# Where attention weights are normalised in a hybrid decoder layer: from GpSimd to VectorE

## The chip, the cores and the metric

One core of a Trainium2 chip. The metric is the device time of one execution in microseconds (us). A difference of about 0.2% (1.2 us) is what a measurement of this kernel can tell from no change; this bound is used throughout. Engines are named as the profile names them: PE (TensorE; PEld is its weight load), DVE (VectorE), ACT (ScalarE), POOL (GpSimd), SP (SyncE, which issues most transfers).

## What is computed

One decoder layer for 512 tokens of width 1024, in fp32. Token mixing projects the normalised input into two groups of eight heads of 64: group A is block-sparse attention (with 512 tokens and blocks of 256, every query sees all earlier keys), group B is a sliding window of 128 with a learned sink per head. The outputs are joined, projected, normalised and gated; a squared-ReLU MLP of 4096 hidden units follows. What matters here is the softmax of one head and one block of 128 queries:

```python
# group A: causal, up to 512 keys
p = softmax(q @ k.T * scale + bias)
# group B: two blocks of 128 keys, and one more column, the sink, whose weight is thrown away
p = softmax(concatenate([where(allowed, q @ k.T * scale + bias, -inf), sink]))[..., :-1]
out = p @ v
```

## The kernel before, in words

The layer is three stages in the span. Up to about 80 us the first normalisation, the conditioning vectors and the first q and k projections. From 80 to 232 us attention, with the remaining projections and the output projection mixed in. From 232 us the residual, the second normalisation and the MLP, which is a nearly unbroken run of matmuls to the end.

**Attention.** There are 64 blocks (`blocks`, line 822): eight pairs of heads, two heads each, four blocks `i` of 128 queries. A block has 128, 256, 384 or 512 keys in the 32 blocks of group A, and 128 (i = 0) or 256 in the 32 of group B (`keys`, line 627). The loop at line 825 is a pipeline over steps k: step k issues the transposes of block k-3, the scores of block k, the normalisation of block k-2, the bias step and the exponentials of block k-1, and the split of the transposed weights of block k-5 or so. For each block:

- `scores` (line 631), PE: two matmuls (lines 641, 642) into a PSUM bank. A tile `w` is taken for the weights, one of four in turn. For group B, POOL copies the head's negated sink into the column behind the last key of `w` (line 640).
- `add_bias` (line 644), DVE: one fused instruction adds the bias strip to the scores, writes `w` and keeps the row minimum in `st` (line 649).
- `exps` (line 653), ACT: the exponential in place, with the row sum in `st` (line 656); with the sink's column for group B.
- `normalise` (line 659): DVE takes the reciprocal of the sum (line 662, 128x1); then POOL multiplies `w` by it (line 663).
- `transposes` (line 665), PE: `w` by 128 columns into PSUM (line 672), the only reader of the normalised weights.
- `weights` (line 674): ACT copies the transposed weights out of PSUM in a rounded form (line 686), DVE takes the difference as the low part (line 687). `output` (line 689) multiplies them with v on PE (line 699); `evacuate` (line 703) uses ACT, DVE and, for a pair of heads, POOL (lines 709 to 715).

**What runs beside it.** `side_steps` (line 786) sums 24 tiles of conditioning weights (512 KB each) in 48 instructions on DVE (lines 282, 284), two a tile, spread over the steps by `side_at` (line 795). Weights are split in a high part by ACT (line 83) and a low part by POOL, in some cases by DVE (line 85). Filler matmuls (projections, then chunks of the output projection, `y_chunk`, line 753) are dealt out between the blocks.

**What sets the order.** PE's order is written out by hand: it is the order of the program (line 821). The other engines are ordered when the program is built, by a planner that simulates the engines and takes what is ready; each engine then runs its queue in that order. Filler and side work is tied behind the latest bias step on DVE and the latest exponential on ACT (`anchor`, `behind`, lines 470 to 477), so it can't be taken earlier; nothing ties it to a latest place.

Of the kernel before, what the change touches and what calls it, by code (L numbers as in the profile page):

```python
# [24 lines left out]
ALU = mybir.AluOpType  # L25
# [7 lines left out]
NHA = 8  # L33
# [13 lines left out]
def layer_kernel(ctx, tc, x, c_col, ada_c, ada_r, bada_col, bada_row, gain_col, gain_row, w_in0, w_in1, w_in2,  # L47
                 w_out, w1, b1_col, w2, b2_row, rel, sinks, onehot, out):
    nc = tc.nc
# [10 lines left out]
    def bank(name):  # L60
        return psum.tile([P, 512], F32, tag="ps", name=name)
# [121 lines left out]
    sink_t = const.tile([P, NHB], F32, name="sink_t")  # L183
# [157 lines left out]
    for i in range(NT):  # L341
        n = DM if i < NT - 1 else S
# [68 lines left out]
    for kc in range(KC):  # L411
# [3 lines left out]
        for k in range(18):  # L415
# [18 lines left out]
            w, h = (w0[kc][0], hh) if k < 6 else (w0[kc][1], hh) if k < 12 else (w0[kc][0], hl)  # L434
# [174 lines left out]
    class Head:  # L609
# [21 lines left out]
        def scores(self, i):  # L631
            k0, nk = self.keys(i)
            n = nk * P
            kk = slice(k0 * P, (i + 1) * P)
            q = self.q[:, i * P:(i + 1) * P]
            self.s[i] = s_ps = bank(f"s{self.h}_{i}")
            tag, bufs = ("stash", 2) if step[0] > 23 and step[0] % 3 == 2 else ("w", 4)
            self.w[i] = w = apool.tile([P, 512], F32, tag=tag, name=f"w{self.h}_{i}", bufs=bufs)
            if self.swa:
                nc.gpsimd.tensor_copy(w[:, n:n + 1], sink_t[:, self.h - NHA:self.h - NHA + 1])  # L640
            nc.tensor.matmul(s_ps[:, :n], q, self.kh[:, kk], start=True, stop=False)
            nc.tensor.matmul(s_ps[:, :n], q, self.kl[:, kk], start=False, stop=True)

        def add_bias(self, i):
            n = self.keys(i)[1] * P
            w = self.w[i]
            self.st[i] = st = small.tile([P, 3], F32, tag="st", name=f"st{self.h}_{i}", bufs=8)
            init = sink_t[:, self.h - NHA:self.h - NHA + 1] if self.swa else BIG
            anchor["dve"] = nc.vector.tensor_tensor_reduce(  # L649
                w[:, :n], self.s[i][:, :n], self.strip[:, 512 - n:], scale=1.0, scalar=init, op0=ALU.add, op1=ALU.min,  # L650
                accum_out=st[:, 0:1]).ins
# [7 lines left out]
        def normalise(self, i):  # L659
            n = self.keys(i)[1] * P  # L660
            w, st = self.w[i], self.st[i]
            nc.vector.reciprocal(st[:, 2:3], st[:, 1:2])  # L662
            nc.gpsimd.tensor_scalar(w[:, :n], w[:, :n], st[:, 2:3], 1.0, op0=ALU.mult, op1=ALU.mult)  # L663

        def transposes(self, i):
            if self.swa and i % 2:
# [368 lines left out]
    for f in range(3, NF):  # L1035
        if f < 5:
            ws.make("both")
        w = ws.get(0 if f < 4 else 1)
# [20 lines left out]
    for f in range(NF - LAST):  # L1059
        w = ws.get()  # L1060
# [106 lines left out]
```

## Time and profile before

| | us |
|---|---|
| median of 3 runs (621.97 to 622.14) | 622.05 |
| the profiled execution's own time | 623.07 |
| its span, first to last instruction | 621.3 |
| PE, DVE, ACT, POOL busy in the span | 580.3, 315.2, 279.2, 321.6 |
| line 663 on POOL, 64 instructions | 38.2 |
| line 640 on POOL, 32 instructions | 11.4 |

The profile is of one execution. Busy time is the time in which an engine has an instruction running; a wait is idle time in front of an instruction, put down to what released it. [...] The execution profiled took 1.8 us more than its span and 1.0 us more than the median of the runs.

### The profile page before, as it was taken

How to read it: one execution, taken by the hardware profiler on the slowest of the kernel's cores; microseconds unless marked ns; L12 is line 12 of the kernel's file. 1: busy time of each engine (PE TensorE's matmuls, PEld its weight loads, DVE VectorE, ACT ScalarE, POOL GpSimd, SP SyncE). 2: the span in 40 equal slices, each digit the busy share in tenths (PEclk: the TensorE clock that was granted, in tenths of full speed). 3: DMA queues.
4: the chain of work that ended last, by engine and by line, in shares of the span. 5: the costliest groups of instructions: out<-in, count | busy, mean ns of one | idle time of the engine just before them, and what ended most of it. 6: DMA issues, size and time to landing. Idle time of an engine off the chain costs nothing.

```text
span 621.3 us, 8137 instructions
## 1 busy us (share of the span) xinstructions
PE 580.3 (93%) x2829; PEld 482.0 (78%) x2829; DVE 315.2 (51%) x599; ACT 279.2 (45%) x532; POOL 321.6 (52%) x333
## 2 busy tenths in 40 slices
PE   2789989999897999999999999999999999999994
PEld 0477889887675888898888888788888888888883
DVE  4646679999998756535255555522401111111037
ACT  4624776578667545773233332233522333323122
POOL 1514234666898653636555555655544444446432
PEclk9969999999998999999999999999999999999998
DMA  8990569686466207734244432223232233333105
GB/s 308 419 383 1 189 129 260 128 170 224 140 185 207 84 1 270 236 106 149 89 136 136 146 125 99 80 93 101 71 112 89 100 103 102 102 101 116 56 17 186
DMA packets 29677, 89.31 MB, mean 144 GB/s; under 512 B 3427, under 2 KB 7587, under 8 KB 29636
## 3 DMA queue, kind: packets, MB, share of 16 engines
q1 hardware_dynamic: 28816, 86.52, 43.5%
q10 hardware_dynamic: 692, 2.23, 0.9%
q8 instruction: 22, 0.36, 0.3%
q14 instruction: 19, 0.16, 0.1%
q0 software_dynamic: 128, 0.05, 0.1%
HBM read 84.56 MB, written 4.22 MB: 143 GB/s over the span
## 4 chain that ended last, share of the span: by engine, by line
PE 55%; DVE 2%; ACT 2%; DMA 1%; issue 1%; POOL 0%; DVEq 0%; POOLq 0%; ACTq 0%; SPq 0%
PE u L97 9%; PE u L98 9%; PE u L96 9%; PE y L98 9%; PE y L97 9%; PE y L96 9%; DVE zg L1090 1%; ACT hf L379 1%; DMA x<-in_x 1%; ACT h2h L378 0%; DVE x L933 0%; DMA out_x<-zg 0%; ACT sq L208 0%; PE adarow L299 0%; POOL zg L1087 0%
## 5 line engine op out<-in xcount | busy, mean ns | idle before, releaser
L85 POOL TENSOR_TENSOR wlo<-raw,whi 128x512 fp32r<-128x512 f32 (+1 forms) x140 | 192.4, 1393 | 157.7 <-ACT whi L83 157.2
L83 ACT ACTIVATE whi<-raw 128x1024 fp32r<-128x1024 f32 (+5 forms) x87 | 80.7, 934 | 130.8 <-PE u L97 108.9
L97 PE MATMUL u<-h2l,whi 128*128 128x512 f32 (+1 forms) x280 | 104.2, 372 | 1.2 <-POOL h2l L380 1.1
L96 PE MATMUL u<-h2h,whi 128*128 128x512 f32 (+1 forms) x280 | 104.7, 374 | 0.0
L98 PE MATMUL u<-h2h,wlo 128*128 128x512 f32 (+1 forms) x280 | 103.8, 371 | 0.0
L97 PE MATMUL y<-wlo,ring_h2h 128*128 128x512 f32 x232 | 90.2, 389 | 0.0
L98 PE MATMUL y<-whi,ring_h2l 128*128 128x512 f32 x232 | 90.2, 389 | 0.0
L96 PE MATMUL y<-whi,ring_h2h 128*128 128x512 f32 x232 | 90.1, 389 | 0.0
L284 DVE SCALAR_TENSOR_TENSOR adaacc<-adar,c_act,adaacc 128x512 f32<-128x512 f32 x56 | 66.7, 1191 | 0.0
L97 PEld LDWEIGHTS u<-h2l,whi 128*128 128x128 f32 x280 | 52.7, 188 | 11.3 <-POOL h2l L380 1.7
L96 PEld LDWEIGHTS u<-h2h,whi 128*128 128x128 f32 x280 | 52.7, 188 | 9.2 <-ACT whi L83 0.2
L98 PEld LDWEIGHTS u<-h2h,wlo 128*128 128x128 f32 x280 | 52.7, 188 | 9.2
L663 POOL TENSOR_SCALAR w<-w,st 128x128 f32<-128x128 f32 (+2 forms) x64 | 38.2, 599 | 38.2 <-DVE st L662 32.8
L97 PEld LDWEIGHTS y<-wlo,ring_h2h 128*128 128x128 f32 x232 | 43.5, 188 | 9.1
L96 PEld LDWEIGHTS y<-whi,ring_h2h 128*128 128x128 f32 x232 | 43.5, 188 | 9.0
L98 PEld LDWEIGHTS y<-whi,ring_h2l 128*128 128x128 f32 x232 | 43.5, 188 | 9.0
L656 ACT ACTIVATE w<-w,st 128x128 f32<-128x128 f32 (+3 forms) x64 | 33.4, 522 | 28.2 <-DVE st L649 26.1
L85 POOL TENSOR_TENSOR w0lo<-w0raw,w0hi 128x384 fp32r<-128x384 f32 x16 | 17.2, 1095 | 29.3 <-ACT w0hi L83 29.3
L672 PE MATMUL p<-ident,w 128*128 128x128 f32 x136 | 25.9, 279 | 6.4 <-POOL w L663 5.9
L672 PEld LDWEIGHTS p<-ident,w 128*128 128x128 f32 x136 | 17.3, 142 | 13.4 <-POOL w L663 9.6
L686 ACT ACTIVATE pth<-p 128x384 fp32r<-128x384 f32 (+3 forms) x48 | 22.2, 466 | 10.1 <-PE p L672 9.6
L687 DVE TENSOR_TENSOR ptl<-p,pth 128x384 fp32r<-128x384 f32 (+3 forms) x48 | 25.0, 523 | 0.8 <-ACT pth L686 0.6
(222 smaller groups left out, 1093.9 us busy)
## 6 DMA issues: line engine op xcount, KB each, us to landing
raw<-in_w SPq DMA_DIRECT2D x63, 512.0 KB, 3.3
adar<-in_ada_r SPq DMA_DIRECT2D x32, 512.0 KB, 4.1
ada<-in_ada_c SPq DMA_DIRECT2D x16, 512.0 KB, 8.6
woraw<-in_w_out SPq DMA_DIRECT2D x8, 512.0 KB, 4.4
raw<-in_w_in SPq DMA_DIRECT2D x7, 512.0 KB, 6.7
w0raw<-in_w_in SPq DMA_DIRECT2D x8, 384.0 KB, 9.1
strip<-vec SPq DMA_DIRECT2D x24, 128.0 KB, 4.1
xn<-in_x SPq DMA_DIRECT2D x4, 512.0 KB, 10.0
```

Of the source, the lines that this page charges most:

```text
L83: nc.scalar.activation(hi[:, a:b], src[:, a:b], AF.Copy)
L85: return eng.tensor_sub(lo[:, a:b], src[:, a:b], f32(hi[:, a:b])).ins
L96: nc.tensor.matmul(ps, lh, rh, start=start, stop=False, **kw)
L97: nc.tensor.matmul(ps, lh, rl, start=False, stop=False, **kw)
L98: nc.tensor.matmul(ps, ll, rh, start=False, stop=stop, **kw)
L284: nc.vector.scalar_tensor_tensor(a, w, c_act[:, j:j + 1], a, op0=ALU.mult, op1=ALU.add)
L379: nc.scalar.activation(hf[:, :n], tp, AF.Identity, bias=sh_col, scale=a_col)
L656: anchor["act"] = nc.scalar.activation(w[:, :m], w[:, :m], AF.Exp, bias=st[:, 0:1], scale=-1.0, accum_out=st[:, 1:2]).ins
L663: nc.gpsimd.tensor_scalar(w[:, :n], w[:, :n], st[:, 2:3], 1.0, op0=ALU.mult, op1=ALU.mult)
L672: nc.tensor.transpose(p_ps[:, (c0 + j) * P:(c0 + j + 1) * P], self.w[i][:, j * P:(j + 1) * P], ident)
L686: nc.scalar.activation(dst(self.pth), src, AF.Copy)
L687: nc.vector.tensor_sub(dst(self.ptl), src, f32(dst(self.pth)))
```

## The change

In `scores` the copy of the sink's column by POOL goes. In `add_bias` the same copy is issued on DVE, directly ahead of the bias step. In `normalise` the multiplication is issued on DVE, directly behind the reciprocal. Shapes, operands and everything else stay.

```diff
--- before.py
+++ after.py
@@ -636,8 +636,6 @@
             self.s[i] = s_ps = bank(f"s{self.h}_{i}")
             tag, bufs = ("stash", 2) if step[0] > 23 and step[0] % 3 == 2 else ("w", 4)
             self.w[i] = w = apool.tile([P, 512], F32, tag=tag, name=f"w{self.h}_{i}", bufs=bufs)
-            if self.swa:
-                nc.gpsimd.tensor_copy(w[:, n:n + 1], sink_t[:, self.h - NHA:self.h - NHA + 1])
             nc.tensor.matmul(s_ps[:, :n], q, self.kh[:, kk], start=True, stop=False)
             nc.tensor.matmul(s_ps[:, :n], q, self.kl[:, kk], start=False, stop=True)
 
@@ -646,6 +644,8 @@
             w = self.w[i]
             self.st[i] = st = small.tile([P, 3], F32, tag="st", name=f"st{self.h}_{i}", bufs=8)
             init = sink_t[:, self.h - NHA:self.h - NHA + 1] if self.swa else BIG
+            if self.swa:
+                nc.vector.tensor_copy(w[:, n:n + 1], init)
             anchor["dve"] = nc.vector.tensor_tensor_reduce(
                 w[:, :n], self.s[i][:, :n], self.strip[:, 512 - n:], scale=1.0, scalar=init, op0=ALU.add, op1=ALU.min,
                 accum_out=st[:, 0:1]).ins
@@ -660,7 +660,7 @@
             n = self.keys(i)[1] * P
             w, st = self.w[i], self.st[i]
             nc.vector.reciprocal(st[:, 2:3], st[:, 1:2])
-            nc.gpsimd.tensor_scalar(w[:, :n], w[:, :n], st[:, 2:3], 1.0, op0=ALU.mult, op1=ALU.mult)
+            nc.vector.tensor_scalar(w[:, :n], w[:, :n], st[:, 2:3], 1.0, op0=ALU.mult, op1=ALU.mult)
 
         def transposes(self, i):
             if self.swa and i % 2:
```

## Rows read from the trace of the kernel before

**Rows 1.** Busy time by stretch of the span, all engines of the core:

```profile
core 0: us, PE busy (x) PEld busy (x) DVE busy (x) ACT busy (x) POOL busy (x), PEclk, DMA share, GB/s
...
90.00:110.00 20.00, 18.74 (x129) 18.16 (x130) 19.86 (x59) 14.53 (x42) 9.21 (x12) 1.00 0.86 212
110.00:150.00 40.00, 39.99 (x214) 33.24 (x212) 38.39 (x90) 27.84 (x71) 27.10 (x30) 1.00 0.75 181
150.00:190.00 40.00, 34.36 (x200) 28.37 (x201) 39.40 (x107) 29.25 (x77) 34.35 (x54) 1.00 0.56 167
190.00:200.00 10.00, 7.06 (x32) 4.70 (x31) 8.59 (x22) 7.55 (x15) 7.94 (x11) 0.89 0.59 188
200.00:210.00 10.00, 10.00 (x53) 8.70 (x52) 6.68 (x23) 3.90 (x12) 6.95 (x14) 0.77 0.62 184
210.00:232.00 22.00, 22.00 (x131) 18.88 (x131) 14.26 (x40) 13.60 (x32) 12.75 (x25) 1.00 0.01 1
```

**Rows 2.** Waits of PE from 80 to 232 us (total, times, longest in us):

```profile
PE p L672 <- POOL w L663: 5.9, 8, 1.6
PE y L97 <- POOL wo_hl L85: 1.7, 2, 1.3
```

**Rows 3.** Timeline, all engines, around one SWA block (start us, us taken):

```profile
168.87 0.19 ACT L656 ACTIVATION_READ_ACCUMULATOR w<-w,st 128x1 f32 x1
...
169.23 0.67 DVE L687 TENSOR_TENSOR ptl<-p,pth 128x512 fp32r<-128x512 f32 x1
...
169.82 0.67 DVE L710 TENSOR_TENSOR of<-o,of 64x512 f32<-64x512 f32 x1
...
170.52 0.69 DVE L528 SCALAR_TENSOR_TENSOR q<-proj,q 64x512 fp32r<-64x512 f32 x1
...
171.05 1.29 POOL L85 TENSOR_TENSOR wlo<-raw,whi 128x512 fp32r<-128x512 f32 x1
...
171.24 0.35 DVE L649 CUSTOM_DVE_ANT_0 w<-s,strip,sink_t 128x128 f32<-128x128 f32 x1
...
171.52 1.36 DVE L284 SCALAR_TENSOR_TENSOR adaacc<-adar,c_act,adaacc 128x512 f32<-128x512 f32 x1
...
172.80 0.15 DVE L662 RECIPROCAL st<-st 128x1 f32<-128x1 f32 x1
...
173.06 0.48 POOL L663 TENSOR_SCALAR w<-w,st 128x256 f32<-128x256 f32 x1
...
173.59 0.44 PE L672 MATMUL p<-ident,w 128*128 128x128 f32 x2 [0.63 <-POOL w L663]
```

**Rows 4.** POOL's groups by shape from 80 to 200 us, the change's two lines:

```profile
L663 POOL TENSOR_SCALAR w<-w,st 128x256 f32<-128x256 f32 x20 | 11.1, 556 | 7.5 <-DVE st L662 4.0 <-PE v L97 3.0
L640 POOL COPY w<-sink_t 128x1 f32<-128x1 f32 x21 | 9.0, 438 | 1.7 <-PE p L672 1.7
...
L663 POOL TENSOR_SCALAR w<-w,st 128x512 f32<-128x512 f32 x8 | 7.5, 940 | 8.1 <-DVE st L662 8.0
L663 POOL TENSOR_SCALAR w<-w,st 128x128 f32<-128x128 f32 x13 | 6.7, 518 | 12.5 <-DVE st L662 12.4
L663 POOL TENSOR_SCALAR w<-w,st 128x384 f32<-128x384 f32 x8 | 5.2, 648 | 6.1 <-DVE st L662 4.6 <-PE p L672 1.4
```

**Rows 5.** VectorE's groups by shape, 0 to 30 us, line 337:

```profile
L337 DVE TENSOR_SCALAR xn<-xn,s2x 128x128 f32<-128x128 f32 x4 | 1.1, 286 | 1.2 <-POOL s2x L213 1.2
```

**Rows 6.** Instructions of line 282 (ns: least, median, most):

```profile
L282 DVE TENSOR_SCALAR adaacc<-adar,c_act x8: 477/896/1512, 51.3 to 319.3; 128x512 f32<-128x512 f32 x8
```

**Rows 7.** Timeline of VectorE, a producer and the instruction that reads it:

```profile
15.47 0.15 DVE L256 TENSOR_TENSOR mods<-adaps,bada_c 128x2 f32<-128x2 f32 x1
15.66 0.21 DVE L259 TENSOR_SCALAR mods<-mods,gain_c 128x1 f32<-128x1 f32 x1
```

**Rows 8.** Timeline of VectorE, four small instructions that don't depend:

```profile
163.50 0.57 DVE L259 TENSOR_SCALAR mods<-mods,gain_c 128x1 f32<-128x1 f32 x4
```

**Rows 9.** Busy time of line 85 from 80 to 200 us, VectorE, then POOL:

```profile
80.00:200.00 120.00, 8.72 (x10) 29.07 (x22) 0.99 0.67 177
```

**Rows 10.** VectorE's groups by shape from 80 to 200 us, the side products:

```profile
L284 DVE SCALAR_TENSOR_TENSOR adaacc<-adar,c_act,adaacc 128x512 f32<-128x512 f32 x39 | 38.5, 987 | 0.0
...
L282 DVE TENSOR_SCALAR adaacc<-adar,c_act 128x512 f32<-128x512 f32 x4 | 3.3, 847 | 0.0
```

**Rows 11.** Instructions of line 284 (ns: least, median, most):

```profile
L284 DVE SCALAR_TENSOR_TENSOR adaacc<-adar,c_act,adaacc x56: 724/1059/1881, 54.0 to 395.5; 128x512 f32<-128x512 f32 x56
```

## The prediction, made before the changed kernel was run

> **What bounds the kernel now.** I read the busy time by stretch first, because shares over the whole span mix attention with an MLP that the change doesn't touch. Attention has two parts [rows 1]. From 110 to 150 us PE is busy 39.99 of 40 us: the matmuls set the pace. From 150 to 190 us PE is busy 34.36 of 40, and from 190 to 200 us 7.06 of 10; its granted clock then falls to a mean of 0.89 and 0.77 in the two stretches around 200 us. What must be seen beside it is DVE: 19.86 of 20 us, 38.39 of 40, 39.40 of 40. From 90 to 190 us it has 2.35 us free in 100. POOL is busy too, 34.35 of 40 us, but only late.
>
> The waits of PE name POOL: 5.9 us in 8 waits are put down to line 663 [rows 2]. The timeline shows what lies behind such a wait [rows 3]. ACT has the row sum ready at 169.06 us (168.87 + 0.19). The reciprocal starts at 172.80, 3.74 us later, because DVE first works off its queue: lines 687, 710, 528, 649, 284. POOL then starts 0.11 us after the reciprocal and takes 0.48 us, and PE goes on at 173.59, having idled 0.63 us. So the releaser is POOL, but 3.74 of the 4.53 us from row sum to transposes are DVE's queue. In attention DVE is the engine without room, and after 232 us nothing is left that could make up for a late end, as PE runs matmuls nearly without a gap.
>
> A second thing is in the same rows. Line 284 on DVE took 1.36 us there; its least is 0.72 [rows 11]. It began at 171.52, in the middle of POOL's line 85 (171.05 to 172.34), and ended 0.54 us after that. DVE instructions with their operands in SBUF wait out the POOL instruction that they meet.
>
> **What is removed.** POOL loses line 663, 30.5 us in 49 instructions from 80 to 200 us, and line 640, 9.0 us in 21 [rows 4]. POOL doesn't set the pace, so by itself this gives nothing; what it gives is shorter waits of DVE, below. The hop to POOL goes from the chain of a block: 0.11 + 0.48 us become about 0.04 + 0.35. That is latency, and with a queue of 3.7 us in front of it, it doesn't matter.
>
> **The multiplication on DVE.** No row shows this line on DVE; the nearest are the same operation of the same form on other tiles: 286 ns for 128x128 [rows 5], 477 ns for 128x512 when nothing interferes [rows 6]; between them I go in a straight line, 0.35 and 0.41 us for 256 and 384. An independent instruction starts about 0.08 us before the end of the one in front: four of 0.20 us stand in 0.57 us [rows 8]. So each costs the queue 0.20, 0.27, 0.33 or 0.40 us, and the 13, 20, 8 and 8 of the stretch [rows 4] 2.6 + 5.4 + 2.6 + 3.2 = 13.8 us. The multiplication reads the reciprocal just in front of it. A reader starts 0.04 us behind its producer's end [rows 7] and not 0.08 us before it, 0.12 us more; for 49 that is 5.4 us with the rounding, unless the planner puts another instruction between. Bounds 13.8 and 19.2 us; I take the middle, 16.5, since both orders will occur.
>
> [...]
>
> **The sink's copy on DVE.** No row shows it; the nearest are 128x1 instructions, one every 0.12 us [rows 8]. 21 of them make 2.5 us; 1.5 if each costs only the 0.07 us between a reciprocal and the start of an independent instruction behind it, 6.7 if each also meets POOL as below. It waits for the `w` buffer to be free, as the bias step behind it did already, so no wait is new. I take 2.5.
>
> **Meeting POOL.** The multiplication moves from POOL onto DVE as an instruction that POOL can hold up: line 282, the same operation, has a median of 896 ns against a least of 477 [rows 6]. What stays on POOL from 80 to 200 us is line 85, 29.1 us in 22 [rows 9], and some 10 us of other work (POOL's 78.6 us from 90 us on [rows 1] less lines 85, 663 and 640): 39 of 120 us. Half a piece of line 85 is 0.66 us; the rest is in shorter pieces, and I take 0.60 for all. One in three meets a piece and waits 0.60 us, so 0.20 us each, 9.8 us for 49. Bounds: nothing, if they never meet, and 0.42 us each, 20.6 us, if they fare like line 282's median.
>
> **What DVE gets back.** Lines 284 and 282 took 38.5 us in 39 and 3.3 us in 4 [rows 10]; at their least, 0.72 and 0.48, that would be 28.2 and 1.9, so 11.7 us were waits for POOL. A wait goes with the length of what is met: lines 663 and 640 (0.62 and 0.44 us long) carry 30.5 x 0.31 + 9.0 x 0.22 = 11.5, the rest 39 x 0.60 = 23.4, so a third, 3.8 us, goes. Bounds 0 and 11.7.
>
> **The sum.** 16.5 + 2.5 + 9.8 - 3.8 = 25.0 us more work on DVE by 200 us, less its 2.35 us of free time: 23 us later. Two things come back. The 1.7 us in which PE waits for POOL's halves of the output weights [rows 2] end, as POOL is less loaded. [...] Of these 5.1 us I take 4: 19 us. The other 15 multiplications and 11 copies fall after 200 us, where DVE is busy 6.68 of 10 and 14.26 of 22 us [rows 1]; their 15 x 0.34 + 11 x 0.12 = 6.4 us I cost at nothing, since 11 us are free there and PE sets the pace; without that cover they'd be 6 us more. The delay then runs to the end one to one: from a profiled time of 623.07 us to 642, from the median of 622.05 us to 641. With all low ends the sum is 13.8 + 1.5 + 0 - 11.7 - 2.35 - 5.1 = -3.9 us, with all high ends 19.2 + 6.7 + 20.6 - 2.35 = 44.
>
> **The rivals.** *Faster: the hop was the limit.* If DVE's queue isn't what holds PE, the shorter chain ends PE's 5.9 us of waits for line 663 and the 3.4 us of low clock: 9.3 us less, 613 us. It decides at the transposes of the group B blocks from 150 us on, and needs that DVE has room there. For it: the waits name POOL, and POOL is busy 34.35 of 40 us. Against it: the 3.74 us in which the row sum lay ready [rows 3]. 0.07. [...]
>
> *Covered.* The planner orders DVE anew. If it pushes the side products of lines 282 and 284, which nobody needs before the second normalisation, behind the blocks' own work, or if nearly all waits for POOL vanish, the added work finds room: -4 to +3 us, 622. Against it: the side product starts right behind a bias step [rows 3], as soon as its tie allows. 0.08, of which 0.05 lies within 0.2%.
>
> *Much slower.* The multiplications meet POOL as line 282's median does, 10.8 us more, and PE, idle more often, falls to its lower clock twice more at the 3.4 us that it cost here: 19 + 10.8 + 6.8, 658 us. For it: 7.06 busy of 10 us stand in front of the fall [rows 1]; against it: 34.36 of 40 did not bring one. 0.11.
>
> **How the numbers follow.** The forecast, DVE's queue paces attention, has 0.74 and spans +5 to +33 us by its own bounds taken half way. The range 627 to 655 us leaves out the faster case, the covered one and half of the heaviest, 0.2 in all. Faster by over 0.2%: 0.07. Within: 0.05. Slower: the rest, 0.88.
>
> **What would show it.** In the changed profile DVE should be busy 98% from 90 us to past 210, line 663 on DVE should have means over the uncontended 0.29 to 0.48 us, with 0.1 to 0.3 us of waiting in each. PE should wait at line 672 for DVE, some 25 us in many small waits instead of 5.9, and the first transposes of group B's last head should come some 19 us later, with the MLP unchanged in length. POOL's line 85 should stay near its length. I'd be wrong if DVE had free time between 110 and 190 us, if line 284 stood far behind its bias steps, or if the end of attention stayed near 232 us.

## The result and the profile after

The changed kernel takes 639.04 us (median of 4 runs, 638.91 to 639.55) against 622.01 us for the kernel before beside it: 17.0 us more, a ratio of 1.0289 with a 95% interval from 1.0259 to 1.0319. (The ratio is formed from all runs and is not the quotient of the two medians, which is 1.0274; the same holds below.) The profiled execution took 639.05 us, its span is 637.3.

The first view is the page's busy time by engine (us, share of the span, instructions).

```profile
PE 584.1 (92%) x2829; PEld 482.7 (76%) x2829; DVE 338.5 (53%) x695; ACT 279.8 (44%) x532; POOL 273.6 (43%) x237
```

DVE reads 338.5 us against 315.2 before, POOL 273.6 against 321.6: VectorE has 23.3 us more work, POOL 48.0 us less. The same stretches as in [rows 1], now of the kernel after (PEclk is the clock that TensorE was granted, as a share of its full one):

```profile
core 0: us, PE busy (x) PEld busy (x) DVE busy (x) ACT busy (x) POOL busy (x), PEclk, DMA share, GB/s
...
90.00:110.00 20.00, 17.49 (x115) 15.75 (x116) 19.43 (x56) 12.17 (x34) 2.92 (x3) 1.00 0.85 209
110.00:150.00 40.00, 36.98 (x199) 30.46 (x198) 39.48 (x94) 24.28 (x61) 14.66 (x14) 1.00 0.66 152
150.00:190.00 40.00, 32.22 (x176) 26.62 (x175) 39.43 (x122) 26.44 (x67) 13.67 (x12) 0.96 0.50 147
190.00:200.00 10.00, 7.95 (x45) 6.04 (x43) 9.81 (x27) 6.36 (x18) 5.19 (x5) 1.00 0.50 138
200.00:210.00 10.00, 6.21 (x30) 4.99 (x31) 9.81 (x29) 6.59 (x16) 1.85 (x2) 0.91 0.42 123
210.00:232.00 22.00, 20.40 (x115) 16.45 (x114) 21.39 (x73) 13.11 (x32) 8.20 (x9) 0.96 0.43 141
```

VectorE was full until 190 us before and had 3.32 of 10 and 7.74 of 22 us free behind it. It is full to 232 us now: 9.81 of 10, 9.81 of 10, 21.39 of 22. TensorE, at 39.99 of 40 us from 110 to 150 before, is at 36.98: it waits there now too. The granted clock is at 0.50 from 177.5 to 180.9 and from 208.3 to 211.7 us, where it was at 0.50 from 197.8 to 204.6 us before, and at 1.00 elsewhere in attention; back-to-back matmuls of 512 columns mostly start 0.43 us apart at 0.50 and 0.23 at 1.00. By the means of the stretches that costs an estimated 40 x 0.04 + 10 x 0.09 + 22 x 0.04 = 3.4 us of matmul time, as much as the 10 x 0.11 + 10 x 0.23 = 3.4 us before [rows 1], so the clock doesn't account for the difference.

How much of the 16.0 us of span arose in attention is read from a step that both chains of waits contain, the first residual step behind attention (line 933). Before, then after:

```profile
249.36 2.82 DVE x L933 x2
```

```profile
265.71 2.46 DVE x L933 x2
```

16.35 us of delay are there at 265.71 us, and 16.0 us at the end of the span. The MLP kept its length. Who holds TensorE in attention (total, times, longest):

```profile
PE p L672 <- DVE w L663: 12.8, 12, 2.2
PE p L672 <- DVE st L662: 2.6, 1, 2.6
PE y L97 <- DVE wloo L85: 1.8, 1, 1.8
PE p L672 <- DVE w L648: 1.7, 1, 1.7
```

The 5.9 us in 8 waits of [rows 2] have become 12.8 + 2.6 + 1.7 us in 14 waits, now put down to VectorE. The halves of the output weights, 1.7 us behind POOL before, are waited for behind VectorE's own splitting (1.8 us). VectorE's groups by shape over attention, 80 to 260 us:

```profile
L284 DVE SCALAR_TENSOR_TENSOR adaacc<-adar,c_act,adaacc 128x512 f32<-128x512 f32 x40 | 33.6, 840 | 0.0
L663 DVE TENSOR_SCALAR w<-w,st 128x256 f32<-128x256 f32 x32 | 15.7, 491 | 0.3
...
L663 DVE TENSOR_SCALAR w<-w,st 128x384 f32<-128x384 f32 x8 | 6.1, 762 | 0.1
L663 DVE TENSOR_SCALAR w<-w,st 128x128 f32<-128x128 f32 x16 | 6.0, 374 | 0.1
...
L663 DVE TENSOR_SCALAR w<-w,st 128x512 f32<-128x512 f32 x8 | 4.7, 585 | 0.1
L648 DVE COPY w<-sink_t 128x1 f32<-128x1 f32 x32 | 4.4, 138 | 0.0
...
L282 DVE TENSOR_SCALAR adaacc<-adar,c_act 128x512 f32<-128x512 f32 x4 | 3.9, 1008 | 0.0
```

Four things are in it. The 64 multiplications take 15.7 + 6.1 + 6.0 + 4.7 = 32.5 us. At the durations without interference of the prediction (0.29, 0.35, 0.41, 0.48 us) they would take 16 x 0.29 + 32 x 0.35 + 8 x 0.41 + 8 x 0.48 = 23.0; the other 9.5 us, 0.15 us each, are meetings with POOL. The trace bears that out: the 42 that overlap no instruction of POOL take at most 0.29, 0.36, 0.41 and 0.49 us, and the 22 that overlap one carry the excess. The 32 copies take 4.4 us, of which about half overlaps with what is behind them. Line 284 is down to 840 ns in the mean, from 987 [rows 10]: 40 x 0.147 = 5.9 us that VectorE got back from POOL, as 28 of the 40 now overlap no instruction of POOL, where 8 did not before. Line 282 got nothing back (1008 ns in the mean, 847 before [rows 10]). An instruction's time overlaps with that of its neighbours (behind the multiplication at 205.10 us, which takes 0.35 us, the next instruction starts at 205.36), so these rows add up to more than the 23.3 us of busy time.

### The profile page after: what moved, and what is told of

Read it like the earlier page. It is cut to its first block, busy times and chain, and to the rows that moved or that the text cites. A ratio compares the mean times of both kernels' runs of the same rounds, so it can differ in the third digit from the quotient of the medians.

```text
span 637.3 us, 8053 instructions
## 1 busy us (share of the span) xinstructions
PE 584.1 (92%) x2829; PEld 482.7 (76%) x2829; DVE 338.5 (53%) x695; ACT 279.8 (44%) x532; POOL 273.6 (43%) x237
## 4 chain that ended last, share of the span: by engine, by line
PE 53%; DVE 2%; ACT 2%; DMA 1%; issue 1%; POOL 0%; DVEq 0%; POOLq 0%; ACTq 0%; SPq 0%
PE u L97 9%; PE u L98 9%; PE u L96 9%; PE y L98 9%; PE y L97 9%; PE y L96 9%; DVE zg L1090 1%; DMA x<-in_x 1%; ACT hf L379 1%; ACT h2h L378 0%; DMA out_x<-zg 0%; DVE x L933 0%; ACT sq L208 0%; PE adarow L299 0%; POOL zg L1087 0%
## 5 line engine op out<-in xcount | busy, mean ns | idle before, releaser
L97 PEld LDWEIGHTS u<-h2l,whi 128*128 128x128 f32 x280 | 52.7, 188 | 11.5 <-POOL h2l L380 1.9
L284 DVE SCALAR_TENSOR_TENSOR adaacc<-adar,c_act,adaacc 128x512 f32<-128x512 f32 x56 | 60.8, 1086 | 0.1
L672 PE MATMUL p<-ident,w 128*128 128x128 f32 x136 | 26.1, 281 | 18.3 <-DVE w L663 12.8
L663 DVE TENSOR_SCALAR w<-w,st 128x128 f32<-128x128 f32 (+2 forms) x64 | 32.0, 507 | 0.5
L1027 DVE TENSOR_TENSOR ring_h2l<-rsq_hl,ring_h2h 128x512 fp32r<-128x512 f32 x8 | 5.5, 694 | 38.0 <-ACT ring_h2h L1026 38.0
```

The costliest lines, as they stand in the source:

```text
L97: nc.tensor.matmul(ps, lh, rl, start=False, stop=False, **kw)
L284: nc.vector.scalar_tensor_tensor(a, w, c_act[:, j:j + 1], a, op0=ALU.mult, op1=ALU.add)
L663: nc.vector.tensor_scalar(w[:, :n], w[:, :n], st[:, 2:3], 1.0, op0=ALU.mult, op1=ALU.mult)
L672: nc.tensor.transpose(p_ps[:, (c0 + j) * P:(c0 + j + 1) * P], self.w[i][:, j * P:(j + 1) * P], ident)
```

## The experiments

Each kernel ran beside the kernel before on the same chip. The kernel before had medians of 621.3 to 621.5 us there, its single runs from 617.8 to 624.4. The intervals reach 0.2 to 0.35%, some 1.3 to 2.1 us, to either side.

**One part at a time.** The copy alone (the multiplication stays on POOL):

```diff
     def scores(self, i):
...
-            if self.swa:
-                nc.gpsimd.tensor_copy(w[:, n:n + 1], sink_t[...])
     def add_bias(self, i):
...
+            if self.swa:
+                nc.vector.tensor_copy(w[:, n:n + 1], init)
```

> Only the sink's copy goes to VectorE, the multiplication stays on POOL. If VectorE's amount of work is the cost: 32 copies at 0.07 us between starts are 2.4 us more, less about 1 us of waits for POOL's copies that end: 0 to +2 us against before. If POOL's late queue was what held TensorE (its copies took 9.0 us from 80 to 200 us): 3 to 5 us faster than before.

Measured: 619.78 us, ratio 0.9977 (0.9955 to 1.0). That lies below the range of the first theory and above that of the second; it is at the edge of no change. The gain of 3 to 5 us is just excluded (the interval ends at 2.8 us).

The multiplication alone:

```diff
     def normalise(self, i):
...
-            nc.gpsimd.tensor_scalar(w[:, :n], w[:, :n], st[:, 2:3], 1.0, op0=ALU.mult, op1=ALU.mult)
+            nc.vector.tensor_scalar(w[:, :n], w[:, :n], st[:, 2:3], 1.0, op0=ALU.mult, op1=ALU.mult)
```

> Only the multiplication goes to VectorE, the sink's copy stays on POOL. If VectorE's amount of work is the cost: +14 to +17 us against before, nearly all of the change's 17. If the copy, by tying the start of the bias step to VectorE's queue, had a large part: under +12 us.

Measured: 635.29 us, ratio 1.022 (1.0199 to 1.0242), 13.9 us more than the 621.39 beside it, just under the first theory's range, which its interval reaches. The multiplication is most of the change. The parts don't add up: -1.6 and +13.9 against +17. With the multiplication in place the copy costs 639.04 - 635.29 = 3.7 us (from runs that did not stand beside each other), alone nothing. The profiles explain most of it: beside the multiplication the copy adds 2.8 us to VectorE's busy time (338.5 against 335.7), alone 0.4 (315.6 against 315.2), where line 284 gets faster with it, from 987 to 944 ns. The rest was not traced.

**Room on VectorE.** 42 of the 48 side products left out, in the kernel after and in the kernel before:

```diff
     def ada_wide(r, pool, then):
...
-                else:
+                elif r == 3:
                     nc.vector.scalar_tensor_tensor(a, w, c_act[:, j:j + 1], a, op0=ALU.mult, op1=ALU.add)
```

> The changed kernel with 42 of the 48 side products on VectorE left out (three of the four vectors of conditioning weights are then incomplete; their transfers stay). If VectorE's amount of work is the cost, taking some 30 us of it away frees the stage: the time falls by 22 to 30 us to 609 to 617, and lies within 4 us of the kernel before with the same work left out. If the cost is the place of the multiplication in the queue (a latency of each block), the time stays 10 us or more above that kernel.

> The kernel before with the same 42 side products left out. If VectorE was already the bound from 150 us on: 8 to 12 us faster than before (TensorE's idle time of 5.6 and 2.9 us and 3.4 us of low clock), no more, since TensorE then sets the pace. If POOL was the bound there: within 4 us of before.

Measured: 615.42 us for the kernel after, 23.6 less than with its side products, and 609.31 for the kernel before, 12.1 less. The fall and the time of the first are as the theory of the amount had them, and the second is at the end of its range. But the change still costs 6.1 us in this pair: fewer than 17, yet not within the 4 of the one theory, nor the 10 of the other. Where the 6 us arise, the busy time from 150 to 210 us shows (columns as above). After, without the products:

```profile
150.00:190.00 40.00, 34.69 (x199) 28.78 (x198) 38.46 (x133) 29.23 (x73) 16.62 (x16) 1.00 0.31 96
190.00:200.00 10.00, 8.64 (x52) 7.17 (x52) 9.96 (x35) 6.12 (x16) 5.06 (x6) 1.00 0.53 170
200.00:210.00 10.00, 9.20 (x59) 8.01 (x58) 9.83 (x38) 7.36 (x19) 2.37 (x3) 1.00 0.01 2
```

Before, without them:

```profile
150.00:190.00 40.00, 36.79 (x215) 30.58 (x214) 32.79 (x100) 31.55 (x79) 32.61 (x60) 1.00 0.38 117
190.00:200.00 10.00, 10.00 (x64) 8.74 (x63) 8.03 (x27) 6.38 (x18) 6.65 (x16) 1.00 0.28 90
200.00:210.00 10.00, 10.00 (x63) 8.64 (x62) 7.58 (x26) 7.60 (x19) 8.58 (x15) 1.00 0.00 0
```

With the products gone the blocks of group B follow each other faster (215 matmuls from 150 to 190 us, where the kernel before had 200), and the multiplications bring VectorE back to 38.46 of 40, 9.96 and 9.83 of 10 us in this stretch; before they ran on POOL and VectorE had 32.79, 8.03 and 7.58. So the room was used up again there, and hardly anywhere else: from 110 to 150 us TensorE is full in both (39.85 and 40.00 of 40 us). The 12.1 us of the kernel before say that VectorE did hold it, as the prediction had read from [rows 3]; they include the 3.4 us of low clock, which is gone (1.00 throughout).

**No multiplication at all.**

```diff
             nc.vector.reciprocal(st[:, 2:3], st[:, 1:2])
-            nc.gpsimd.tensor_scalar(w[:, :n], w[:, :n], st[:, 2:3], 1.0, op0=ALU.mult, op1=ALU.mult)
+            pass
```

> The kernel before with the multiplication left out on every engine (the weights stay unnormalised). If VectorE's amount of work sets the time: VectorE gets back what it waited for POOL's multiplications, 4 to 7 us, so 2 to 7 us faster than before, and the changed kernel lies 19 to 24 us above this one. If the hop to POOL was the limit: 9 us or more faster than before.

Measured: 620.76 us, ratio 0.9997 (0.9974 to 1.002). POOL's 64 multiplications and their hop cost the kernel before nothing that can be measured, so there was nothing to win by moving them. The 2 to 7 us from VectorE's shorter waits didn't show either, and the kernel after lies 18.3 us above this run, just under the expected 19 to 24. The busy time from 150 to 200 us:

```profile
150.00:190.00 40.00, 35.40 (x200) 29.39 (x201) 39.37 (x110) 30.27 (x78) 22.91 (x34) 0.99 0.58 177
190.00:200.00 10.00, 8.68 (x36) 7.10 (x36) 7.51 (x20) 5.89 (x14) 7.22 (x9) 0.71 0.61 183
```

VectorE is as full as before up to 190 us (39.37 of 40). The clock doesn't hide a gain: at 0.99 and 0.71 it costs an estimated 0.4 + 2.9 = 3.3 us here, as in [rows 1]. But VectorE got back less than expected: it is busy 312.7 us in the span against 315.2, 2.5 us less and not 4 to 7, and up to 1.6 us of gain would lie within the interval.

**The same amount of work, in nobody's way.** The multiplication stays on POOL; VectorE multiplies a spare tile that nothing reads:

```diff
             nc.gpsimd.tensor_scalar(w[:, :n], w[:, :n], st[:, 2:3], 1.0, op0=ALU.mult, op1=ALU.mult)
+            for a in range(0, n, 256):
+                x = spare[:, :min(256, n - a)]
+                nc.vector.tensor_scalar(x, x, mhalf, 1.0, op0=ALU.mult, op1=ALU.mult)
```

> The kernel before, and on VectorE beside POOL's multiplication one of the same shape on a spare tile that nobody waits for (two for 384 and 512 columns). If VectorE's amount of work is the cost: 64 blocks at 0.20 to 0.54 us make 20 us, 10 to 15 us of waits for POOL come on top, less 10 to 16 us of free time: +15 to +25 us, although no block waits for these instructions. If the place of the multiplication in a block's chain is the cost: within 5 us of before.

Measured: 642.2 us, ratio 1.0336 (1.0307 to 1.0364), 20.9 us more than beside it. Two of its stretches:

```profile
110.00:150.00 40.00, 35.04 (x188) 28.90 (x187) 39.56 (x100) 23.53 (x61) 20.86 (x24) 1.00 0.61 154
...
210.00:232.00 22.00, 18.85 (x92) 15.29 (x92) 21.69 (x58) 9.95 (x24) 14.01 (x23) 0.84 0.48 150
```

VectorE is full and TensorE falls back as in the kernel after (35.04 of 40 and 18.85 of 22 us). No block waits for these instructions. VectorE is busy 342.3 us in the span, 27.1 more than before, and the span grew by 20.0 (641.3 against 621.3): 7.1 us went into free time, as 7.3 did in the kernel after. This is the run that decides between the theories: amount of work on a full engine is enough to make the delay. Not all of the 20.9 us is VectorE's time alone: the granted clock is 0.973 in the mean over this span, 0.983 before and 0.982 in the kernel after, so the lower clock takes an estimated 641.3 x 0.027 = 17.3 us here, against 10.6 and 11.5. How much of that is paid was not separated.

**The place in the queue.** In 54 of the 64 blocks the planner doesn't put the multiplication directly behind its reciprocal. Part of VectorE's timeline of the kernel after:

```profile
205.10 0.35 DVE L663 TENSOR_SCALAR w<-w,st 128x256 f32<-128x256 f32 x1
205.36 0.68 DVE L687 TENSOR_TENSOR ptl<-p,pth 128x512 fp32r<-128x512 f32 x1
...
206.80 0.16 DVE L662 RECIPROCAL st<-st 128x1 f32<-128x1 f32 x1
206.88 0.13 DVE L648 COPY w<-sink_t 128x1 f32<-128x1 f32 x1
206.93 1.22 DVE L85 TENSOR_TENSOR wloo<-woraw,whio 128x1024 fp32r<-128x1024 f32 x1
208.18 0.35 DVE L649 CUSTOM_DVE_ANT_0 w<-s,strip,sink_t 128x128 f32<-128x128 f32 x1
...
208.45 1.52 DVE L284 SCALAR_TENSOR_TENSOR adaacc<-adar,c_act,adaacc 128x512 f32<-128x512 f32 x1
210.00 0.70 DVE L710 TENSOR_TENSOR of<-o,of 64x512 f32<-64x512 f32 x1
210.73 0.17 DVE L662 RECIPROCAL st<-st 128x1 f32<-128x1 f32 x1
210.81 0.45 DVE L663 TENSOR_SCALAR w<-w,st 128x256 f32<-128x256 f32 x1
```

The reciprocal at 206.80 belongs to the block whose multiplication starts at 210.81, 3.85 us after the reciprocal's end; the copy, a split of weights, a bias step, a side product and an output step stand between. Over the 64 blocks it is 1.1 us in the mean; before, POOL's multiplications started 0.67 us behind the reciprocal in the mean. Whether that costs something by itself was tried by tying each bias step behind the multiplication issued just ahead of it in the program:

```diff
+            anchor["norm"] = nc.vector.tensor_scalar(w[:, :n], w[:, :n], st[:, 2:3], 1.0, ...).ins
...
         if h:
-            h.add_bias(i)
+            with tc.issue_after(anchor["norm"]) if "norm" in anchor else ExitStack():
+                h.add_bias(i)
```

> The changed kernel with each bias step tied behind the multiplication of the block before it, so that the planner can't put the multiplication so far behind its reciprocal (it stands 1.3 us behind in the mean, up to 3.9). If VectorE's amount of work is the cost: within 3 us of the changed kernel, 636 to 642. If the lateness of the multiplication is a cost of its own: 5 us or more faster than the changed kernel.

Measured: 648.48 us, 9.4 more than the kernel after; neither theory had it slower. Its busy time at the end of attention:

```profile
200.00:210.00 10.00, 5.38 (x31) 3.97 (x29) 8.93 (x29) 5.04 (x14) 3.34 (x4) 0.95 0.61 173
210.00:232.00 22.00, 16.07 (x83) 12.67 (x83) 20.77 (x60) 13.19 (x29) 5.52 (x4) 0.87 0.49 156
```

VectorE's amount of work is that of the kernel after (339.3 us busy in the span against 338.5), but now it idles in between, 1.07 of 10 and 1.23 of 22 us here, and TensorE is down to 5.38 and 16.07 us. The multiplications did come forward, to 0.16 us behind their reciprocals in the mean. But by its edit the tie also holds back bias steps that had been free to go, which would explain the idle time; that was not traced. So order matters on a full engine as well, and this run doesn't say what the planner's late places cost; a tie that pulls the multiplication forward and holds nothing else back wasn't found.

**Only where VectorE has room.** The change for steps from 51 on, after some 200 us (the multiplication is shown; the copy goes over at the same step):

```diff
-            nc.gpsimd.tensor_scalar(w[:, :n], w[:, :n], st[:, 2:3], 1.0, op0=ALU.mult, op1=ALU.mult)
+            (nc.vector if step[0] > 50 else nc.gpsimd).tensor_scalar(w[:, :n], w[:, :n], st[:, 2:3], 1.0, ...)
```

> The change for the last blocks alone (from step 51 on, after some 200 us), where VectorE was busy 6.68 of 10 and 14.26 of 22 us. If VectorE's amount of work is the cost: no slower than before, since it has room there, and up to 3 us faster, as POOL's multiplications stood 2.4 to 4.1 us behind their reciprocals around 200 us. If a multiplication on VectorE costs wherever it stands: 3 to 4 us slower (a quarter of the change).

Measured: 621.82 us, ratio 1.0018 (0.9997 to 1.004). The stretches that had room:

```profile
200.00:210.00 10.00, 9.26 (x55) 7.40 (x54) 9.19 (x34) 4.95 (x13) 3.64 (x3) 1.00 0.57 172
210.00:232.00 22.00, 21.11 (x121) 17.38 (x120) 16.17 (x55) 11.72 (x30) 6.64 (x8) 1.00 0.00 1
```

VectorE takes the 15 multiplications and 14 copies, 24 of the 29 behind 200 us, into its free time (9.19 of 10 and 16.17 of 22 us busy, before 6.68 and 14.26) and the time doesn't move measurably; a cost of 3 us or more is excluded. The hoped-for gain of up to 3 us didn't come.

**Moving side work out of the full stretch.** Since leaving the side products out won 12 us, four versions dealt them out more slowly from step 24 on, at 0.5 or 0.35 a step in place of 0.7:

```diff
-        while sided[0] < 4 + min(k, 24) + max(0, min(k, 62) - 24) * 0.7 + max(0, k - 62):
+        while sided[0] < 4 + min(k, 24) + max(0, min(k, 62) - 24) * 0.35 + max(0, k - 62):
```

> The kernel before with the side products dealt out more slowly from step 24 on (0.5 a step in place of 0.7), so that some 5 of them leave the stretch from 150 to 200 us for the free time of VectorE behind it. If VectorE's amount of work in that stretch is what holds the kernel before: 2 to 5 us faster than before. If POOL or the hop is: no change.

> The same with 0.35 a step: some 9 or 10 side products, about 8 us of VectorE, leave the stretch. If VectorE's amount of work is what holds the kernel before: 4 to 8 us faster than before, unless the last products now come late for the second normalisation. If POOL or the hop is: no change.

> The slower pace of 0.35 and the sink's copy alone on VectorE (the multiplication stays on POOL). With the copy alone at 0.9977 of before: within 2 us of the slower pace alone, and the fastest of the four if its small gain adds up.

> The changed kernel with the slower pace of 0.35. If VectorE's amount of work is the cost: 5 to 9 us faster than the changed kernel (630 to 634), since 8 us of VectorE leave its full stretch, but still 6 us or more above before, since the other 14 us of added work stay. If the cost is where the planner puts the multiplication: within 3 us of the changed kernel.

Measured: 621.53 us at 0.5 (ratio 1.001, 0.999 to 1.003), 623.13 at 0.35 (1.0028, 1.0002 to 1.0053), 621.04 with the copy (1.0007, 0.9986 to 1.0029), and 637.8 for the kernel after at 0.35 (1.0251, 1.0217 to 1.0285). The first, the second and the last missed what the first theory expected of them. The third lies 2.1 us below the second, about as expected, but no lower than the kernel before. For the kernel before at 0.35, two stretches, and TensorE's waits in the later one (total, times, longest):

```profile
150.00:190.00 40.00, 37.20 (x217) 30.97 (x215) 36.77 (x109) 32.03 (x84) 32.45 (x57) 1.00 0.43 139
...
210.00:232.00 22.00, 18.80 (x106) 15.08 (x106) 16.82 (x40) 8.42 (x20) 11.18 (x16) 1.00 0.31 96
```

```profile
PE adaps L242 <- DVE of L710: 1.5, 1, 1.5
PE adaps L242 <- DVE ptl L687: 0.6, 1, 0.6
```

From 150 to 190 us it did what was wanted: VectorE 36.77 of 40, TensorE 37.20 (34.36 before). But from 210 to 232 us TensorE is down to 18.80 of 22 where it was full, although VectorE has 5.2 us free there. Of TensorE's 3.2 us, 2.1 are these two waits of line 242, which transposes the sum of the side products: the last product starts at 228.07 us now, where it started at 201.05 before, behind an output step that had itself waited 3.9 us for ACT. So the exception that the expectation names, products that come late, took part. Why the rest of the gain is missing stays open. For the kernel after at 0.35:

```profile
200.00:210.00 10.00, 6.75 (x39) 5.13 (x37) 9.81 (x27) 6.51 (x16) 5.03 (x5) 1.00 0.54 157
210.00:232.00 22.00, 20.05 (x119) 16.72 (x119) 21.78 (x71) 14.38 (x37) 6.34 (x7) 1.00 0.29 91
```

Up to 232 us there is no free time behind 200 us into which work could go (9.81 of 10, 21.78 of 22), so the expectation's premise was false there; from 232 to 250 us TensorE waits at line 242 for the late products here too, 2.1 us. By its own number, within 3 us of the kernel after, this run fits the theory of the place; the spare multiplications speak for the amount. A version faster than both kernels was not found.

## Why the prediction was right

The forecast was +19 us in a range of +5 to +33; measured +17.0. Its mechanism, VectorE's queue paces attention and work added where it is full is paid, is shown by four runs: spare work in nobody's way costs 20.9 us, work taken away wins 12.1 and 23.6 us, and a quarter of the change, in VectorE's free time, costs nothing that can be measured. The order within the full queue stays open: the tie cost 9.4 us, and the side products dealt out more slowly won nothing. That the number came within 2 us is in part luck, since two errors offset each other. By its steps:

- **VectorE's added work, over-sized.** The sum had 25.0 us up to 200 us and 6.4 behind, 31.4 in all; the page shows 23.3. The multiplications without interference are as forecast: the first in the timeline above, with 256 columns, holds VectorE from 205.10 to 205.36 us, 0.26 us, where the forecast had 0.27. The reader's place behind its producer (2.7 us, half of 5.4, where 49 x 0.12 would be 5.9) hardly arose: in 10 of 64 blocks. Meetings with POOL were put at 0.20 us each and measured 0.15: one in three met an instruction of POOL, as forecast, but waited 0.43 us (9.5 us in 22) and not 0.60. The copies were put at 0.12 us each, the rate of other 128x1 instructions; the next instruction starts 0.08 us behind the copy's start in the mean (206.88 to 206.93 in the timeline above), near the low bound. And VectorE got back more than the 3.8 us forecast: 5.9 us on line 284.
- **Free time.** 23.3 us of work lengthened the span by 16.0, so 7.3 us went into time that VectorE had free. The prediction used 2.35 + 6.4 = 8.75 us of it; it left out the 1.41 us free from 190 to 200 us [rows 1].
- **What comes back besides, 4 us.** This step failed. The wait for the output weights did not end but went over to VectorE's splits (1.8 us in place of 1.7), and the other 3.4 of its 5.1 us, which are the clock column of [rows 1], 10 x 0.11 + 10 x 0.23, recurred as low clock elsewhere, an estimated 3.4 us again. The error is hidden in the total, since the added work was put too high by twice as much, 8.1 us.
- **The hop.** The prediction let it shrink from 0.59 to 0.39 us, read from one block. In the mean over all blocks the way from the reciprocal's end to the multiplication's start grew, from 0.67 to 1.1 us, by the planner's order. It was right that the hop wasn't the limit: without any multiplication the time is the same.
- **The chain's tell-tales.** VectorE full to past 210 us, a delay of some 19 us at attention's end (16.35), the MLP unchanged, many small waits at line 672: all there, the waits with 17 us in place of 25.
- **The range.** Its bounds are called half the way to -3.9 and 44 us; that would be +7.6 and +31.5, so +5 and +33 are a little wider. The measured time lies within both.

Taken alone, the multiplication is faster on VectorE: 256 columns take 0.33 to 0.36 us there with no instruction of POOL beside them and took 0.56 us in the mean on POOL [rows 4]. Yet the kernel is 2.9% slower, since VectorE was full.

## What to carry to other kernels

The releaser that a wait names can be the last step of a chain and not its cause (here POOL, where 3.74 of the 4.53 us lay in VectorE's queue [rows 3]): go back from it to where the data lay ready, and see whose queue it lay in. Price a move between engines by the target's free time in the very stretch, and count the moved work in full where there is none, even if no one waits for it: of the 23.3 us that the change added to VectorE here the span paid 16.0, and of the 27.1 us of spare multiplications 20.0. And when work is to be moved out of a full stretch, check first that the place it goes to is free in the kernel at hand (with the change VectorE had 0.19 of 10 and 0.22 of 22 us there), and that nothing there waits for the moved work (2.1 us at line 242).

## What the runs showed of the hardware beyond that

The two moved instructions behave differently beside POOL. The copy of one column and the multiplication, in nanoseconds (least, median, most), kernel after:

```profile
L648 DVE COPY w<-sink_t x32: 122/140/154, 162.4 to 235.4; 128x1 f32<-128x1 f32 x32
```

```profile
L663 DVE TENSOR_SCALAR w<-w,st x64: 261/355/1529, 82.9 to 239.9; 128x256 f32<-128x256 f32 x32, 128x128 f32<-128x128 f32 x16, 128x384 f32<-128x384 f32 x8, 128x512 f32<-128x512 f32 x8
```

A copy and a multiplication that both started while the second of two instructions of POOL ran (the row joins the two):

```profile
176.31 2.61 POOL L85 TENSOR_TENSOR wloo<-woraw,whio 128x512 fp32r<-128x512 f32 x2 [2.37 <-ACT whio L83]
...
177.71 0.14 DVE L648 COPY w<-sink_t 128x1 f32<-128x1 f32 x1
177.77 1.29 DVE L663 TENSOR_SCALAR w<-w,st 128x256 f32<-128x256 f32 x1
```

The multiplication ends at 179.06 us, 0.14 us behind the end of POOL's instruction (178.92). The copy, wholly inside the same instruction, takes its usual 0.14 us. The 32 copies lie between 122 and 154 ns, with none drawn out, though both their operands are in SBUF. Only 6 of them ran wholly within an instruction of POOL; in the run with the copy alone 20 of 32 did, and they took 133 to 154 ns. The multiplications range from 261 to 1529 ns, a few of them held for nearly a whole POOL instruction. So the prediction's sentence that VectorE's instructions with operands in SBUF wait out the POOL instruction they meet does not hold for the copies. It holds for most of the multiplications: 19 of the 22 that overlap an instruction of POOL end 0.08 to 0.28 us behind the end of one, and the other three, which began 0.06 to 0.09 us ahead of POOL's, took 0.27 to 0.42 us. In the kernel before it holds for 36 of the 47 instructions of line 284 that overlap one of POOL: they end 0.53 to 0.55 us behind the end of one. The other 11 took 0.72 to 0.75 us, about as long as the 9 that overlap none (0.74 to 0.75); one of them, at 185.88 us, ran wholly within a copy of POOL's line 640. Line 649, whose scores lie in PSUM, took 0.67 to 0.69 us for 512 columns, seven times beside POOL and once not.
